# Down's first product evacuated by ScalarE and the residual added later; low parts of weights behind their casts; state sums behind state updates

## The chip, the cores and the metric

The kernel runs on one core of a Trainium2 chip. The metric is the time on the device of one execution of the whole program, in microseconds (us); the median of several runs is taken. A core has five engines, each with its own stream of instructions that it executes in order: TensorE (PE in the profile; its weight loads are PEld), VectorE (DVE), ScalarE (ACT), GpSimd (POOL) and SyncE (SP). Here SP issues nearly all the transfers (DMAs) between the chip's main memory and the on-chip memory SBUF. Matmuls write into PSUM, from where ACT or DVE bring the results back.

## The reference

One layer of a hybrid decoder on 1040 prompt tokens (16 of them learned) and 8 sample tokens, 1048 columns in all, model width 1024, float32:

```
h  = h + 0.5 * swiglu(rmsnorm(h, n1), w1g, w1u, w1d)          # FFN1, hidden width 2816
u  = rmsnorm(h, nm) @ w_in                                    # q, f, i, g (HGRN2); z, x, B, C, dt (Mamba-2)
o  = hgrn2 scan over 4 heads of 128, rms-normed per head, times silu(g)
y  = ssd scan over 8 heads of 64 with state 128, gated by silu(z), rms-normed in two groups
h  = h + concat(o, y) @ w_out
h  = h + 0.5 * swiglu(rmsnorm(h, n2), w2g, w2u, w2d)          # FFN2
y  = rmsnorm(h, norm_final)
swiglu(x, wg, wu, wd) = (silu(x @ wg) * (x @ wu)) @ wd
```

For each of the 8 samples the states of both scans are read, advanced by one token and written out: `h_t = exp(dt A) h + dt x B^T`, `y = h_t C + D x` for the Mamba-2 part, with a state of 512 x 128 per sample.

## The kernel before

**Products.** Every large matmul multiplies float32 numbers as two parts: a high part rounded to fp32r by a cast on ACT, and a low part, the difference, by a subtraction on DVE (`split`, lines 135 to 138). `mm3` (lines 140 to 145) issues three matmuls a product: high by high, high by low, low by high. Columns are handled in quarters of Q = 262.

**The two FFNs** (`ffn`, with `pair` for gate and up, `down` for Down) are written as blocks of 2 x 2 with seven products instead of eight. The seven products are sums and differences of blocks of weights and operands; they are taken in the order 1, 6, 2, 5, 7, 3, 4 in gate and up and 1, 5, 6, 7, 3, 4, 2 in Down. Their order in time is written out by hand: a list of steps (`Steps`), each of which holds some matmuls and perhaps an evacuation after them, and `S.before(i, fn)` puts other work (loads, sums, casts, low parts) ahead of step i in program order. PE, DVE, ACT and SP keep that order here; each engine still runs as far ahead as its waits let it.

*Gate and up.* Each of 22 pairs has 14 steps of 12 matmuls. `Left` prepares its weights: `load` issues four DMAs into tiles of tag "r" (8 buffers), `sum_` makes three sums and differences on DVE, `hi` casts on ACT and `lo` subtracts on DVE into a tile of tag "ws" (6 buffers). `Left.plan` gives the steps, counted from the pair's first: the loads at -10 and -9, the sums at -7 to -5, the split of the i-th product at 2i - 4 (one later for the second pair). `post` evacuates: product 7 makes u1 and multiplies it by the spread factors of the norm (`times_r`, line 445), product 3 does so with g1 and then applies SiLU.

*Hidden.* After every two pairs the hidden blocks and their differences are stored to main memory (`Hidden.jobs`, line 538, tiles of tag "s", 8 buffers).

*Down.* Seven products of 24 steps each: four groups j of 256 output rows, each of three groups g of hidden blocks (4, 4 and 3), each of two halves c. An evacuation follows each j. Operands come back from main memory into tiles of tag "u" (30 buffers; `Hidden.load`: the DMA into the low tile, cast at line 559, low part at line 563), 12 tiles a product, at steps 2, 5, 8, 11, 14 and 17 of the product before. Weights: `pieces` loads 13 steps ahead (line 596), sums 9 ahead (line 606), casts 8 ahead (line 611) and makes the low part 7 ahead (line 616). Six "u" tiles keep sums of weights from product 5 to product 3. The old h of each of the eight row blocks (524 KB) is loaded by `load_h` (line 581) into a tile of tag "s", at steps -4, 2, 8 and 9 for two blocks each, from the copy `xT` in FFN1. `post` adds 0.5 times each finished product to that tile on DVE (line 634). Product 1 goes into all four parts of a j, products 5, 6, 7, 3, 4 and 2 into two, three, two, one, one and one.

Accumulators in the FFNs: two PSUM tiles of two banks each. PE can fill one while the other is evacuated.

**The middle** (input projection, SSM scan, HGRN2 heads, output projection) is not ordered by hand: a scheduler places the instructions by program order and by its own estimate of when they are ready. `ssm_scan` (lines 1075 on) is a chain over nine chunks of 128 tokens; during it PE works at the projections of the first head (`hgrn_project`: q, f, v). Each projected chunk of 350 columns is evacuated by ACT with its function at once: SiLU for q (line 1256), two sigmoids for f (lines 1260 and 1261), a copy for v (line 1266). The scan's own ACT work is Relu and Exp (lines 1111, 1112, 1121). ACT has to load a table of functions when it changes between these sets (ACT_TABLE_LOAD). After each of q, f and v, three jobs are taken from a list: one job per sample (`ssm_samples`), eight of them, and `skip`. A job loads the sample's state, decays it and adds the update on POOL (lines 1191, 1195, 1196), and reduces it against C on DVE (line 1198) right after; then SP stores it (line 1199).

`ssm_norm` squares two tiles on ACT (lines 1231, 1232), adds them on POOL (1233), sums over partitions by matmuls with ones (1237) and scales. For the second group it stands ahead of the output projection's first part (`out_proj`, lines 1459 on), whose operands come back from main memory (line 1718) and are split (lines 137, 138).

Of the kernel before, what the change touches and what calls it, by code (L numbers as in the profile page):

```python
# [17 lines left out]
P = 128  # L18
# [5 lines left out]
NS = 8  # L24
# [318 lines left out]
class Left:  # L343
# [83 lines left out]
def pair(K, S, wg, wu, f, ops, spread, hid, first=None):  # L427
# [20 lines left out]
    def post(p, cs, b):  # L448
        if p == 1:
            nc.scalar.copy(temp("z", cs), b)  # L450
        elif p == 6:
            nc.vector.tensor_add(temp("v", cs), b, temp("z", cs))
        elif p == 2:
            t = times_r("g0", 0, cs, b)
            nc.scalar.activation(t, t, AF.Silu)  # L455
        elif p == 5:
            nc.vector.tensor_add(temp("x", cs), b, temp("v", cs))
        elif p == 7:
            nc.vector.tensor_add(temp("u1", cs), b, temp("x", cs))
            times_r("u1", 1, cs)  # L460
        elif p == 3:
            nc.vector.tensor_add(temp("g1", cs), b, temp("v", cs))
            t = times_r("g1", 1, cs)
            nc.scalar.activation(t, t, AF.Silu)  # L464
        else:
            nc.vector.tensor_add(temp("u0", cs), b, temp("v", cs))
            times_r("u0", 0, cs)
            if "h" not in tm:
                tm["h"] = True
                hid.append(K.slot("s", T))  # L470
            for n in range(2):
                nc.vector.tensor_mul(halves(hid[0][:, n * 2 * Q : n * 2 * Q + 2 * Q])[:, cs], temp(f"g{n}", cs), temp(f"u{n}", cs))
# [8 lines left out]
    def post_first(p, cs, b):  # L481

        if p in (5, 2):
            late[p] = b
        elif p == 7:
            nc.vector.tensor_add(temp("u1", cs), b, temp("x", cs))
        elif p == 3:
            post(2, cs, late[2])
            post(3, cs, b)
            times_r("u1", 1, cs)  # L490
        else:
            post(p, cs, b)
            if p == 6:
                post(5, cs, late[5])
# [77 lines left out]
def down(K, S, wdv, hidden, src, h, after):  # L572
# [576 lines left out]
def ssm_samples(K, a, o):  # L1149
# [34 lines left out]

    def sample(b):
        sb = K.raw().rearrange("p (j n) -> p j n", j=4)
# [5 lines left out]
        for g in range(2):  # L1192
# [3 lines left out]
            nc.gpsimd.tensor_add(sb[:, j2], sb[:, j2], up)  # L1196
            for j in (2 * g, 2 * g + 1):
                nc.vector.tensor_tensor_reduce(up[:, j % 2], sb[:, j], rows[:, 2 + g], 1.0, 0.0, ALU.mult, ALU.add, ys[:, j, b : b + 1])
# [6 lines left out]
    return [lambda b=b: sample(b) for b in range(NS)] + [skip]  # L1205

# [19 lines left out]
def ssm_norm(K, g, tag):  # L1226

    nc = K.nc
    ya, yb = K.y[2 * g], K.y[2 * g + 1]
    v, r = K.slot(tag, w=T), K.slot(tag, w=T)  # L1230
    nc.scalar.activation(v, ya, AF.Square)
    nc.scalar.activation(r, yb, AF.Square)
    nc.gpsimd.tensor_add(v, v, r)
    for c0, w in CHUNKS:
# [13 lines left out]
def hgrn_project(K, a, hd, which, jobs=3):  # L1248
# [9 lines left out]
    def ev_f(c0, w, ps):  # L1258
        f, k = out["f"][:, c0 : c0 + w], out["k"][:, c0 : c0 + w]
        nc.scalar.activation(f, ps, AF.Sigmoid)  # L1260
        nc.scalar.activation(k, ps, AF.Sigmoid, scale=-1.0)
        nc.vector.tensor_scalar(f, f, oml, lb, ALU.mult, ALU.add)
# [302 lines left out]
def body(ctx, tc, a, o):  # L1565
# [130 lines left out]
    for hd in range(NH):  # L1696
        u = hgrn_project(K, a, hd, "qfv")
        pieces = hgrn_scan(K, a, o, hd, u)
        if hd == 0:
            ssm_gate(K, a, 0)  # L1700
            ssm_norm(K, 0, "s")
            for i in range(2):
# [23 lines left out]
    out_proj(K, a, h, 0, opa, 0)  # L1726
    opb = []
# [130 lines left out]
```

## Time and profile before

| | |
|---|---|
| median of 3 runs | 2137.22 us (2134.08 to 2138.86) |
| the profiled execution's own time | 2141.21 us |
| its span, first to last instruction | 2139.4 us |
| mean granted clock of TensorE | 0.975 |
| PE busy | 2021.8 us, 15495 matmuls |
| DVE, ACT, POOL busy | 1491.7, 803.0, 141.3 us |
| HBM read and written | 191.26 and 65.47 MB, 120 GB/s over the span |

Where the stages lie in the span: FFN1's gate and up to 507 us, its Down to about 765, the input projection of the SSM part to about 870, the scan to about 980, the heads to about 1295, the output projection to about 1425, FFN2's gate and up to 1876, its Down to the end.

How to read it. The page gives each engine's busy time and share of the span. A group row (`line engine op out<-in ...`) gives busy time and the mean duration in ns, and behind the second bar the idle time of that engine just ahead of the group with what ended it. A waits row says who waited for whom: us in total, times, the longest. A row by stretches gives from:to, its length, then busy time and number of instructions of PE, PEld, DVE, ACT and POOL, the granted clock, the share of the 16 DMA engines and GB/s. A row of the chain gives start, duration and what ran. Matmuls overlap each other, so the mean duration of one is longer than the distance between two.

### The profile page before, as it was taken

The page shows a single profiled execution, that of the slowest core. Times are in us where ns is not written, and L with a number is a line of the kernel's source. Part 1 is how long each engine was busy: PE and PEld are TensorE (multiplying, and loading weights), DVE is VectorE, ACT ScalarE, POOL GpSimd, SP SyncE. Part 2 cuts the span into 40 slices and gives each one's busy share as a digit, 9 for nine tenths or more (in the row PEclk, how much of TensorE's full clock was granted, in tenths as well). Part 3 has the DMA queues.
Part 4 walks back from the last instruction along what each step waited for, and adds up shares of the span by engine and source line. Part 5 has one row for each costly group of instructions (what it writes and reads, how often), then busy time and mean ns, then how long its engine had stood idle before and what let it go on. Part 6 is the DMA issues. An engine that isn't in the chain of part 4 may idle for free.

```text
span 2139.4 us, 38417 instructions
## 1 busy us (share of the span) xinstructions
PE 2021.8 (95%) x15495; PEld 1965.4 (92%) x15495; DVE 1491.7 (70%) x2489; ACT 803.0 (38%) x1494; POOL 141.3 (7%) x175
## 2 busy tenths in 40 slices
PE   5999999999899899799999998979999999989996
PEld 5999999999899889788989997979999999989996
DVE  6777777777787676596454366677777777778863
ACT  7422222223335443562432335652222222324342
POOL 1000000000002110321111010220000000000000
PEclk8999999999999999999999999999999999999999
DMA  6323333246956511452022053313233242587651
GB/s 189 89 81 100 103 93 105 78 131 228 295 165 194 155 47 31 119 154 75 32 71 79 2 176 107 103 60 106 88 107 105 76 120 81 172 265 230 208 166 59
DMA packets 325033, 259.17 MB, mean 121 GB/s; under 512 B 17712, under 2 KB 301104, under 8 KB 324848
## 3 DMA queue, kind: packets, MB, share of 16 engines
q1 hardware_dynamic: 324616, 256.68, 39.5%
q8 instruction: 122, 2.00, 0.4%
q14 instruction: 55, 0.45, 0.1%
q0 software_dynamic: 224, 0.04, 0.0%
q10 hardware_dynamic: 16, 0.00, 0.0%
HBM read 191.26 MB, written 65.47 MB: 120 GB/s over the span
## 4 chain that ended last, share of the span: by engine, by line
PE 78%; DVE 8%; DMA 6%; ACT 3%; issue 2%; SPq 1%; POOL 1%; DVEq 0%; ACTq 0%; POOLq 0%
PE acc L143 24%; PE acc L144 23%; PE acc L145 23%; DMA r<-in_w_ffn_down_dram 2%; DMA r<-in_w_ffn_up_dram 2%; PE mis L1355 2%; DMA u<-hd 1%; DVE s L634 1%; DVE u L287 1%; DVE r L360 1%; PE mis L1394 0%; PE mis L1450 0%; DVE ws L616 0%; DVE u L298 0%; PE mis L1412 0%
## 5 line engine op out<-in xcount | busy, mean ns | idle before, releaser
L143 PE MATMUL acc<-u,ws 128*128 128x262 f32 (+2 forms) x4504 | 1326.9, 296 | 56.5 <-DVE s L634 20.1
L144 PE MATMUL acc<-u,ws 128*128 128x262 f32 (+2 forms) x4504 | 1315.6, 292 | 0.6 <-DVE u L563 0.3
L145 PE MATMUL acc<-u,ws 128*128 128x262 f32 (+2 forms) x4504 | 1313.9, 292 | 1.0 <-DVE ws L368 0.8
L143 PEld LDWEIGHTS acc<-u,ws 128*128 128x128 f32 x4504 | 858.2, 191 | 75.1 <-issue 21.7
L144 PEld LDWEIGHTS acc<-u,ws 128*128 128x128 f32 x4504 | 862.4, 191 | 2.5 <-DVE u L563 0.7
L145 PEld LDWEIGHTS acc<-u,ws 128*128 128x128 f32 x4504 | 858.3, 191 | 1.9 <-DVE ws L368 1.0
L368 DVE TENSOR_TENSOR ws<-r,ws 128x512 fp32r<-128x512 f32 x308 | 212.0, 688 | 103.7 <-ACT ws L364 103.7
L364 ACT CAST ws<-r 128x512 fp32r<-128x512 f32 x308 | 173.3, 615 | 4.7 <-PE acc L145 3.1
L464 ACT ACTIVATE t<-t 128x524 f32<-128x524 f32 (+1 forms) x46 | 28.6, 622 | 313.1 <-DVE t L445 313.1
L360 DVE TENSOR_TENSOR r<-r,r 128x512 f32<-128x512 f32 x176 | 119.1, 697 | 19.0 <-DMA r<-in_w_ffn_up_dram 17.0
L634 DVE SCALAR_TENSOR_TENSOR s<-acc,s 128x524 f32<-128x524 f32 (+1 forms) x120 | 77.6, 663 | 48.8 <-PE acc L145 47.6
L455 ACT ACTIVATE t<-t 128x524 f32<-128x524 f32 (+1 forms) x46 | 28.7, 623 | 216.7 <-DVE t L445 216.7
L204 POOL TENSOR_TENSOR t<-t,t 128x262 f32<-128x262 f32 x56 | 52.9, 960 | 813.2 <-ACT t L203 813.2
L563 DVE TENSOR_TENSOR u<-u,u 128x1048 fp32r<-128x1048 f32 (+1 forms) x84 | 97.1, 1159 | 8.8 <-ACT u L559 8.8
L445 DVE TENSOR_TENSOR t<-t,u 128x524 f32<-128x524 f32 (+1 forms) x138 | 93.6, 681 | 4.7
L138 DVE TENSOR_TENSOR ws<-r,ws 128x512 fp32r<-128x512 f32 x88 | 60.2, 698 | 39.2 <-ACT ws L137 39.0
L611 ACT CAST ws<-r 128x512 fp32r<-128x512 f32 (+1 forms) x84 | 47.8, 581 | 102.9 <-DVE r L606 39.3
L616 DVE TENSOR_TENSOR ws<-r,ws 128x512 fp32r<-128x512 f32 (+1 forms) x84 | 57.2, 691 | 41.6 <-ACT ws L611 41.5
L611 ACT CAST ws<-u 128x512 fp32r<-128x512 f32 (+1 forms) x72 | 42.1, 585 | 113.2 <-DVE u L606 110.9
L559 ACT CAST u<-u 128x1048 fp32r<-128x1048 f32 (+1 forms) x84 | 83.2, 992 | 2.0 <-DMA u<-hd 2.0
L137 ACT CAST ws<-r 128x512 fp32r<-128x512 f32 x88 | 53.8, 617 | 71.7 <-PE acc L145 51.9
L445 DVE TENSOR_TENSOR t<-acc,u 128x524 f32<-128x524 f32 (+1 forms) x46 | 31.3, 680 | 61.6 <-PE acc L145 61.6
(379 smaller groups left out, 1950.1 us busy)
## 6 DMA issues: line engine op xcount, KB each, us to landing
hd<-s SPq DMA_DIRECT2D x170, 262.0 KB
r<-in_w_ffn_down_dram SPq DMA_DIRECT2D x128, 256.0 KB
u<-hd SPq DMA_DIRECT2D x56, 524.0 KB
r<-in_w_ffn_gate_dram SPq DMA_DIRECT2D x88, 256.0 KB
r<-in_w_ffn_up_dram SPq DMA_DIRECT2D x88, 256.0 KB
r<-in_w_in_dram SPq DMA_DIRECT2D x56, 256.0 KB
r<-in_w_ffn_down_dram SPq DMA_DIRECT2D x64, 192.0 KB
u<-hd SPq DMA_DIRECT2D x28, 393.0 KB
```

The lines of the kernel that those rows point to most:

```text
L138: self.nc.vector.tensor_sub(lo, src, hi.bitcast(F32))
L143: mm(ps, whi, xhi, start=first, stop=False, skip_group_check=more)
L144: mm(ps, whi, xlo, start=False, stop=False, skip_group_check=more)
L145: mm(ps, wlo, xhi, start=False, stop=last, skip_group_check=more)
L360: self.K.nc.vector.tensor_tensor(self.raw[p], self.raw[x], self.raw[y], op)
L364: self.K.nc.scalar.copy(self.w[p][:, : self.n * P], self.raw[p])
L368: self.K.nc.vector.tensor_sub(t[:, 512 : 512 + w], self.raw[p], t[:, :w].bitcast(F32))
L445: nc.vector.tensor_mul(t, t if src is None else src, spread.lanes(i, cs))
L559: K.nc.scalar.copy(hi, lo.bitcast(F32))
L563: K.nc.vector.tensor_sub(lo, lo.bitcast(F32), hi.bitcast(F32))
L611: nc.scalar.copy(w[p, j, g][:, : n * P], src)
L634: nc.vector.scalar_tensor_tensor(t, b, 0.5, t, ALU.mult, ALU.add)
```

## The change

Seven edits.

1. `down`: the eight loads of the old h leave the start. Product 1 writes 0.5 times its result with ACT (`nc.scalar.mul`) into new "s" tiles. The old h of block o is loaded into a "u" tile at Down's step 66 + 5o, and added on DVE at step 74 + 5o, that is 66 to 101 and 74 to 109: product 7 has steps 72 to 95, product 3 steps 96 to 119.
2. `Left.plan`: loads one step earlier; the cast stays where it was, and the low part goes one step later.
3. `pair`: the multiplication of u1 goes from behind product 7 to behind product 3's, also in the first pair.
4. `ssm_samples`: a sample's reductions and store go behind the update of the next sample; nine jobs and `skip`, taken four at a time instead of three for the first head.
5. `hgrn_project`, first head: q and f are copied raw out of PSUM chunk by chunk, and the functions run once over all 1048 columns after the third chunk. In `ev_f` the two sigmoids change places.
6. `ssm_norm` ends in a function of its own (`ssm_norm_end`).
7. `out_proj` can call a function after its first quarter (`mid`); the second group's norm is ended there. The first group's is ended at once, as before.

```diff
     def plan(self, S, s0, late):
         for ps, ds, fn in (
-            ((1, 7, 4, 2), (-10, -10, -9, -9), self.load),
+            ((1, 7, 4, 2), (-11, -11, -10, -10), self.load),
             ((5, 6, 7, 3), (-7, -7, -6, -5), self.sum_),
-            (ORDER, [2 * i - 4 + late for i in range(7)], self.split),
+            (ORDER, [2 * i - 4 + late for i in range(7)], self.hi),
+            (ORDER, [2 * i - 3 + late for i in range(7)], self.lo),
         ):
...
         elif p == 7:
             nc.vector.tensor_add(temp("u1", cs), b, temp("x", cs))
-            times_r("u1", 1, cs)
         elif p == 3:
             nc.vector.tensor_add(temp("g1", cs), b, temp("v", cs))
             t = times_r("g1", 1, cs)
             nc.scalar.activation(t, t, AF.Silu)
+            times_r("u1", 1, cs)
...
-    def load_h(o):
-        t = K.slot("s", T)
-        nc.sync.dma_start(t, src(o))
-        h.append(t)
-        hs.append(t.rearrange("p (c n t) -> p c n t", c=2, n=2))
+    def tiles(j):
+        for _ in range(2):
+            h.append(K.slot("s", T))
+            hs.append(h[-1].rearrange("p (c n t) -> p c n t", c=2, n=2))
+
+    def residual(o, at):
+        box = []
+
+        def load():
+            box.append(K.slot("u", T))
+            nc.sync.dma_start(box[0], src(o))
+
+        S.before(at - 8, load)
+        S.before(at, lambda: nc.vector.tensor_add(h[o], h[o], box[0]))
 
     for o in range(KT):
-        S.before(s0 + (-4, 2, 8, 9)[o // 2], lambda o=o: load_h(o))
+        residual(o, s0 + 74 + 5 * o)
...
     def post(p, j, cs, b):
-        for i, n in {1: ((0, 0), (0, 1), (1, 0), (1, 1)), 5: ((0, 1), (1, 1)), 6: ((0, 1), (1, 0), (1, 1)), 7: ((1, 0), (1, 1)), 3: ((0, 1),), 4: ((1, 0),), 2: ((0, 0),)}[p]:
+        if p == 1:
+            tiles(j)
+            for i in range(2):
+                for n in range(2):
+                    nc.scalar.mul(hs[2 * j + i][:, cs, n], b, 0.5)
+            return
+        for i, n in {5: ((0, 1), (1, 1)), 6: ((0, 1), (1, 0), (1, 1)), 7: ((1, 0), (1, 1)), 3: ((0, 1),), 4: ((1, 0),), 2: ((0, 0),)}[p]:
...
-    def sample(b):
+    state = {}
+
+    def update(b):
...
-            for j in (2 * g, 2 * g + 1):
-                nc.vector.tensor_tensor_reduce(up[:, j % 2], sb[:, j], rows[:, 2 + g], 1.0, 0.0, ALU.mult, ALU.add, ys[:, j, b : b + 1])
+        state[b] = sb, rows
+
+    def output(b):
+        sb, rows = state.pop(b)
+        junk = K.t(4 * P).rearrange("p (j n) -> p j n", j=4)
+        for j in range(4):
+            nc.vector.tensor_tensor_reduce(junk[:, j], sb[:, j], rows[:, 2 + j // 2], 1.0, 0.0, ALU.mult, ALU.add, ys[:, j, b : b + 1])
         nc.sync.dma_start(ov[0, b], sb)
+
+    def sample(b):
+        if b < NS:
+            update(b)
+        if b > 0:
+            output(b - 1)
...
+    def ev_raw(x):
+        left = [3]
+
+        def ev(c0, w, ps):
+            nc.scalar.copy(out[x][:, c0 : c0 + w], ps)
+            left[0] -= 1
+            if left[0] == 0:
+                (ev_q if x == "q" else ev_f)(0, T, out[x])
+
+        return ev
...
+    if hd == 0:
+        evs.update(q=ev_raw("q"), f=ev_raw("f"))
...
-def out_proj(K, a, h, part, ops, half, after=None):
+def out_proj(K, a, h, part, ops, half, after=None, mid=None):
...
+        if u == 1 and mid:
+            mid()
...
-        u = hgrn_project(K, a, hd, "qfv")
+        u = hgrn_project(K, a, hd, "qfv", 4 if hd == 0 else 3)
...
-    ssm_norm(K, 1, "u")
+    norm1 = ssm_norm(K, 1, "u")
...
-    out_proj(K, a, h, 0, opa, 0)
+    out_proj(K, a, h, 0, opa, 0, mid=norm1)
```

More of the change, by code (lines that the diff above doesn't have):

```diff
@@ L484, in post_first @@
             late[p] = b
-        elif p == 7:
-            nc.vector.tensor_add(temp("u1", cs), b, temp("x", cs))
         elif p == 3:
@@ L489, in post_first @@
             post(3, cs, b)
-            times_r("u1", 1, cs)
         else:
@@ L1203, in skip @@
             nc.vector.scalar_tensor_tensor(xs[j][:, TP:T], xs[j][:, TP:T], K.dcol[:, j : j + 1], ys[:, j], ALU.mult, ALU.add)
-    return [lambda b=b: sample(b) for b in range(NS)] + [skip]
+    return [lambda b=b: sample(b) for b in range(NS + 1)] + [skip]
 def ssm_gate(K, a, g):
@@ L1226, in ssm_norm, with ssm_norm_end @@
 def ssm_norm(K, g, tag):
-    nc = K.nc
     ya, yb = K.y[2 * g], K.y[2 * g + 1]
     v, r = K.slot(tag, w=T), K.slot(tag, w=T)
-    nc.scalar.activation(v, ya, AF.Square)
-    nc.scalar.activation(r, yb, AF.Square)
-    nc.gpsimd.tensor_add(v, v, r)
+    K.nc.scalar.activation(v, ya, AF.Square)
+    K.nc.scalar.activation(r, yb, AF.Square)
+    K.nc.gpsimd.tensor_add(v, v, r)
+    return lambda: ssm_norm_end(K, g, v, r)
+def ssm_norm_end(K, g, v, r):
+    nc = K.nc
     for c0, w in CHUNKS:
@@ L1259, in ev_f @@
         f, k = out["f"][:, c0 : c0 + w], out["k"][:, c0 : c0 + w]
+        nc.scalar.activation(k, ps, AF.Sigmoid, scale=-1.0)
         nc.scalar.activation(f, ps, AF.Sigmoid)
-        nc.scalar.activation(k, ps, AF.Sigmoid, scale=-1.0)
         nc.vector.tensor_scalar(f, f, oml, lb, ALU.mult, ALU.add)
@@ L1700, in body @@
             ssm_gate(K, a, 0)
-            ssm_norm(K, 0, "s")
+            ssm_norm(K, 0, "s")()
             for i in range(2):
```

## The prediction

> **What bounds the kernel now.** I read the page's busy line, its slices and its chain first, then the waits of PE, then PE's busy time by stage.
>
> ```profile
> span 2139.4 us, 38417 instructions
> PE 2021.8 (95%) x15495; PEld 1965.4 (92%) x15495; DVE 1491.7 (70%) x2489; ACT 803.0 (38%) x1494; POOL 141.3 (7%) x175
> ...
> PE   5999999999899899799999998979999999989996
> ...
> DMA  6323333246956511452022053313233242587651
> ...
> PE 78%; DVE 8%; DMA 6%; ACT 3%; issue 2%; SPq 1%; POOL 1%; DVEq 0%; ACTq 0%; POOLq 0%
> ```
>
> PE is the bound, and all that can be won without taking matmuls away is where it waits. The DMA slices have their high digits at 9 to 11 and 35 to 36: the start of Down in each FFN. Who makes PE wait, in total us, times, longest:
>
> ```profile
> PE acc L143 <- DVE s L634: 21.9, 10, 5.4
> ...
> PE acc L143 <- DVE t L457: 8.2, 7, 6.3
> PE mis L1118 <- DVE s L1114: 7.6, 2, 6.2
> ...
> PE mis L1104 <- DVE s L1125: 5.6, 2, 5.2
> ...
> PE mis L1237 <- POOL u L1233: 4.7, 1, 4.7
> ...
> PE acc L143 <- ACT u L1256: 2.0, 1, 2.0
> ...
> PE acc L143 <- ACT u L1266: 1.7, 1, 1.7
> ...
> PE acc L143 <- DVE t L462: 1.2, 2, 0.6
> ```
>
> L634 is Down's evacuation; L1104 to L1125 are the SSM scan, L1256 and L1266 the first head's projection, L1237 the second SSM norm. Now the busy time by stage. The first row is products 1 and 5 of FFN1's Down, the next three its products 6, 7 and 3; then products 1 and 5 of FFN2, its product 3, and the scan:
>
> ```profile
> 507.50:583.50 76.00, 68.11 (x531) 67.11 (x532) 55.74 (x82) 25.03 (x37) 0.00 (x0) 0.96 0.89 276
> 583.50:615.50 32.00, 32.00 (x265) 32.00 (x264) 27.17 (x42) 12.41 (x18) 0.00 (x0) 1.00 0.54 164
> 615.50:647.50 32.00, 32.00 (x264) 32.00 (x263) 26.81 (x40) 12.42 (x18) 0.00 (x0) 1.00 0.67 207
> 647.50:679.50 32.00, 32.00 (x265) 32.00 (x264) 24.67 (x32) 17.24 (x32) 10.02 (x10) 1.00 0.55 167
> 1875.80:1951.50 75.70, 68.75 (x533) 67.81 (x534) 55.90 (x82) 25.04 (x37) 0.00 (x0) 0.95 0.91 278
> ...
> 2015.50:2047.50 32.00, 32.00 (x265) 32.00 (x264) 22.08 (x32) 14.02 (x21) 0.00 (x0) 1.00 0.67 208
> 880.00:950.00 70.00, 53.67 (x361) 48.06 (x362) 52.74 (x142) 46.09 (x97) 30.57 (x39) 0.90 0.64 185
> ```
>
> A product is 24 steps of 11 matmuls on the average, 264, and takes 32.0 us where nothing is late: 0.121 us a matmul, 1.33 us a step. Products 1 and 5 should take 64.0 us. They take 76.0 and 75.7, of which 3 and 5 matmuls (1.0 us) belong to the neighbours: 22.7 us are lost in the two Downs. PE's idle time is less than that; the granted clock (0.96 and 0.95, against 1.00) is the rest.
>
> Why they are lost, in the stretch 507.5 to 560, by groups, by SP's waits and by the chain:
>
> ```profile
> L143 PE MATMUL acc<-u,ws 128*128 128x262 f32 x113 | 33.5, 297 | 8.1 <-DVE s L634 7.1 <-DVE t L462 0.6 <-ACT ws L611 0.4
> L634 DVE SCALAR_TENSOR_TENSOR s<-acc,s 128x524 f32<-128x524 f32 x16 | 10.9, 700 | 0.3
> L616 DVE TENSOR_TENSOR ws<-r,ws 128x512 fp32r<-128x512 f32 (+1 forms) x9 | 5.7, 643 | 12.1 <-ACT ws L611 12.1
> L611 ACT CAST ws<-r 128x512 fp32r<-128x512 f32 (+1 forms) x9 | 4.9, 582 | 23.3 <-DMA r<-in_w_ffn_down_dram 15.4 <-PE acc L145 7.9
> ...
> SPq L538 <- DVE s L472: 12.1, 1, 12.1
> ...
> 529.70 10.03 DMA r<-in_w_ffn_down_dram
> ...
> s<-xT SPq DMA_DIRECT2D x8, 524.0 KB
> ```
>
> PE waits for L634 (7.1 of 8.1), L634 stands on DVE behind a low part L616, L616 waits for its cast L611, and L611 for a weight's DMA, one of which took 10.03 us for 192 or 256 KB. It stands in line behind the eight residual loads of 524 KB, six of which leave after SP has been held for 12.1 us by the last pair's store.
>
> **The change, part by part.**
>
> *Down's first product.* Out of the start go 8 x 524 KB = 4.2 MB, at 276 GB/s 15 us of transfers, six eighths of it just ahead of the late weights. DVE loses 16 evacuations of 700 ns (10.9 us). ACT gets them; the nearest row, a copy of the same 128x524 from PSUM, is
>
> ```profile
> L450 ACT COPY t<-acc 128x524 f32<-128x524 f32 x17 | 10.2, 597 | 43.6 <-PE acc L145 43.6
> ```
>
> 16 x 0.6 = 9.6 us over product 1, where ACT's own work is about the 12.4 us of the rows of products 6 and 7: it hides. The new waits: evacuations queue on ACT behind casts that wait for weights. A weight of a step s is cast 8 steps (10.7 us) ahead, and PE has two accumulators, so an evacuation may be 8 us late. With 3.1 MB fewer ahead of them (11 us at 276 GB/s) the weights that landed 10 us after issue land in 2 to 5. SP's wait of 12.1 us stays. Of the 22.7 us I leave 1.1 in each Down, for product 5, whose weights come two at a time: -20.5. Ends: 0 and -22.7.
>
> The Trainium skill speaks against this move: "ScalarE: Activation LUTs", Rules for kernel authors, puts mul and add on VectorE. The row disagrees for this shape: ACT 597 ns, DVE 700 ns. At three times DVE's 700 ns, the page's largest ratio, the 16 would be an estimated 34 us, more than product 1 lasts, and the gain would be gone; I go by the row.
>
> *Residual in products 7 and 3.* The eight loads now leave at steps 66 to 101 of Down, eight steps ahead of eight adds at 74 to 109. The add's nearest row is two SBUF operands of 128x1048:
>
> ```profile
> L287 DVE TENSOR_TENSOR u<-u,u 128x1048 f32<-128x1048 f32 x8 | 10.0, 1244 | 0.0
> ```
>
> 9.9 us, 6.2 of it in product 7. DVE has 26.81 of 32 us there: 33.0, over full. But it now idles 0.8 us between a weight's sum and its low part, for ACT's cast, and each add falls between these two; so it falls some 2 us behind, and PE bears up to 8 less the 1 to 2 us that the evacuations trail now. Product 3 has 24.67 + 3.7. Transfers: 207 and 167 GB/s plus 4.2 MB in 47 us (90 GB/s) is below the 276 at which product 5 runs. Buffers: tag "u" has 30 slots. Two products' operands (24) and the kept sums (6) fill them by step 65, so the load at 66 holds SP until PE has done step 66, and with it the weights behind; the operand loads at 86 and 89 are held likewise. SP's lead is set by freed slots already. A weight is loaded 13 steps ahead of PE; held for two, it is still on time. I take +0.5 in each Down, +1.0; ends 0 and the second rival.
>
> *FFN pairs.* Loads go one step (1.33 us) earlier, low parts one step later, still three steps ahead of PE; eight "r" slots hold the seven or eight live ones. DVE's sums wait for a load in 21 pairs:
>
> ```profile
> DVE r L360 <- DMA r<-in_w_ffn_up_dram: 17.0, 21, 1.6
> ```
>
> at most 1.6, so nearly all goes, but PE feels only 8.2 - 6.3 = 1.9 us of it (the 6.3 is FFN2's first pair): -1.5, ends -1.9 and +1. times_r of u1 now follows product 3's g1, so the accumulator that PE wanted at Down's first step is read 0.7 us sooner: L462's 1.2 us go, -1.2. DVE's saved waits for casts lie beside PE: nothing.
>
> *SSM.* Head 0's q and f leave PSUM by copies, with one SiLU and two sigmoids afterwards. Rows of 880 to 950:
>
> ```profile
> L1112 ACT ACT_TABLE_LOAD x4 | 5.1, 1283 | 0.1
> ...
> L1256 ACT ACT_TABLE_LOAD x2 | 2.6, 1283 | 0.0
> L1260 ACT ACT_TABLE_LOAD x2 | 2.6, 1283 | 0.0
> ...
> L1266 ACT COPY u<-acc 128x350 f32<-128x350 f32 x2 | 0.9, 438 | 0.0
> ...
> DVE t L1198 <- POOL r L1196: 9.1, 2, 7.3
> ```
>
> Nine loads (with L1121's) fall to about four: five x 1.283 = 6.4 us off ACT; against it six copies (2.6) and three long calls (3.2) for nine short ones (4.1): 4.7 us net. The Trainium skill ("ScalarE: Activation LUTs", Rules for kernel authors) budgets 2.7 us a switch; by that it would be 11.8 and the whole sum 7 us better; here the row decides. The state sums L1198 move behind the next state's update, so DVE should not stand 7.3 us for POOL. SP's store of each state moves with them. PE's waits here are 7.6 + 5.6 + 2.0 + 1.7 = 16.9. This part isn't ordered by hand, so I take half of the two longest (6.2 and 5.2): -6, ends -16.9 and +6.2 (one more such wait).
>
> *Second norm.* The ones-matmuls go behind the first quarter of the output projection. PE's wait, the norm's six matmuls and the low parts that the quarter needs:
>
> ```profile
> 1297.24 3.59 PE L1237 MATMUL mis<-u,ones 128*128 128x350 f32 x6 [4.70 <-POOL u L1233]
> 1298.21 1.43 DVE u L138 x4
> ```
>
> PE waits from 1292.5 to 1297.2. The first low part is there near 1298.7, so without the norm in front PE would wait about 6 us instead of 4.7, less what ACT and DVE gain by the norm's absence: 0, ends -4.7 and +2.
>
> **Sum.** -20.5 + 1.0 - 1.5 - 1.2 - 6 + 0 = -28.2. The profiled execution took 2141.2: 2113. The median of the three runs is 4.0 lower, so 2109.
>
> **Rivals.** *The first product keeps its waits* (0.10): SP's 12.1 us hold is the cause, and ACT now waits for the weights in DVE's place. For it: the hold stays. Against: DMA runs full after the hold, and most of that is residual. 2109 + 20.5 = 2130, or 2134 if products 7 and 3 pay 2 each.
>
> *Products 7 and 3 pay* (0.17, slower). SP is held for "u" slots at steps 66, 86 and 89, and the weights behind it come late while DVE is full. Price: three waits as long as L634's longest, 5.4; in products 1 and 5 8.1 us of idle time cost 12, so 24 us a Down, 48 - 29 = +19: 2156. It decides from 16.8 us a Down (gains 29.2 and 0.2%, 4.3, halved). Against: product 5 ran with 0.89 DMA share and little loss.
>
> *The scan is ordered worse* (0.09): +6.2 and +2 for -6 and 0: 2123.
>
> **Chances.** The forecast has 0.64. A change of 0.2% (4 us) is about what a measurement can tell. Faster: 0.64 + 0.09 + 0.04 of the first rival = 0.77; same 0.06; slower 0.17. Range: 2094 (the middle at its better ends) to 2138 (both lesser rivals in, the slower one out); the likeliest case alone is 2098 to 2122.
>
> **What would show it.** Right: in Down's products 1 and 5 PE takes about 65 us with granted clock near 1.00, and no weight load takes 10 us; products 7 and 3 stay at 32 each though DVE shows 33 busy; ACT has about four table loads in the scan; PE waits less for L1114 and L1125. Wrong: PE waiting in products 7 or 3 for L634, or SP's longest waits being the residual's; PE waiting for ACT's new evacuation; new scan waits of 5 us.

## The result, and the profile after

The changed kernel takes 2105.28 us (median of four runs, 2096.91 to 2113.13) against 2138.04 for the kernel before on the same chip: a ratio of 0.9843, 95% interval 0.9818 to 0.9868, a gain of 28 to 39 us. Its profiled execution took 2105.23 us, 36.0 less than the one before.

Lines have moved: Down's evacuation L634 is now L647 (product 1's on ACT is L643), the weights' load, sum, cast and low part are L603, L613, L618 and L623, the operand's load, cast and low part L553, L557 and L561, the residual's load and addition L587 and L590. In the scan L1114 and L1125 are L1127 and L1138; the norm's sum and matmul L1258 and L1267.

The page of the changed kernel:

```profile
span 2103.5 us, 38460 instructions
...
PE 2004.5 (95%) x15495; PEld 1951.0 (93%) x15495; DVE 1492.9 (71%) x2469; ACT 819.4 (39%) x1524; POOL 144.7 (7%) x175
...
DMA  6223233336967511452022053313242333487851
```

PE runs the same 15495 matmuls. Its busy time fell by 17.3 us, its idle time by 18.6 (117.6 to 99.0 as span less busy time). A matmul takes less time when the granted clock is higher, and part of the busy time that was won goes with the waits: in Down's products 1 and 5, over both Downs, PE's idle time fell by 14.8 us and its busy time by 7.0, at a granted clock of 0.96 and 0.95 before and 1.00 after. The other 10 us of busy time were won in other stages, most of which the change does not touch; there the clock differs from run to run (see the last paragraph on the prediction). The DMA slices at Down's start (9 to 11, and 35 to 36) are still the fullest.

Who makes PE wait, in total us, times, longest:

```profile
PE acc L143 <- DVE s L647: 9.1, 6, 2.5
...
PE mis L1131 <- DVE s L1127: 7.3, 3, 5.2
...
PE acc L143 <- DVE t L458: 6.6, 2, 6.4
PE mis L1267 <- POOL u L1258: 4.7, 1, 4.7
...
PE acc L143 <- ACT u L1296: 2.6, 1, 2.6
PE acc L143 <- ACT u L1305: 2.0, 1, 2.0
...
PE acc L144 <- DVE u L561: 1.7, 2, 1.2
PE mis L1117 <- DVE s L1138: 1.2, 1, 1.2
```

Down's evacuation went from 21.9 to 9.1 us; the six waits left lie in its last product, which the change did not touch. The 6.4-us wait of FFN2's first pair and the norm's 4.7 us stand as they were, and L462's 1.2 us are gone. In the scan PE waits 8.5 us for the two lines that cost 13.2; nearly all of the fall is L1138's (5.6 to 1.2), while L1127's 7.3 us are close to the 7.6 of before, and the waits for the first head's copies rose from 3.7 to 4.6.

By stretches (length, busy time and count of PE, PEld, DVE, ACT, POOL, clock, DMA share, GB/s): products 1 and 5 of FFN1's Down; its products 7 and 3; products 1 and 5 of FFN2; its product 3:

```profile
504.16:568.50 64.34, 64.34 (x531) 64.34 (x529) 45.31 (x66) 33.68 (x53) 0.00 (x0) 1.00 0.94 271
600.70:632.85 32.15, 32.15 (x266) 32.15 (x265) 28.22 (x41) 11.90 (x17) 0.00 (x0) 1.00 0.73 236
632.85:666.46 33.61, 32.37 (x266) 32.16 (x265) 29.64 (x38) 15.15 (x29) 9.48 (x8) 1.00 0.70 225
1850.20:1914.80 64.60, 64.60 (x530) 64.57 (x529) 45.95 (x67) 33.82 (x53) 0.00 (x0) 1.00 0.92 274
1979.20:2012.00 32.80, 32.38 (x266) 32.17 (x265) 29.25 (x41) 14.52 (x22) 0.00 (x0) 1.00 0.81 260
```

Products 1 and 5 now hold no idle time and run at full clock. Product 3 has 1.24 us of idle time in FFN1 and 0.42 in FFN2.

Where the time went in this and the following kernels. A stage is measured from its first matmul to the next stage's first, so that all kernels are cut at the same matmul; the scan alone is measured from its first transposition to the first of its last group. Each column is one profiled execution; times in us.

| stage | before | after | Down alone | pairs alone | middle alone | loads back | DVE evacuates |
|---|---|---|---|---|---|---|---|
| FFN1 gate and up, without first pair | 434.8 | 431.8 | 435.0 | 432.2 | 435.5 | 433.1 | 433.0 |
| FFN1 Down, product 1 | 40.7 | 32.3 | 32.3 | 40.8 | 41.3 | 40.9 | 33.1 |
| product 5 | 34.9 | 32.1 | 32.1 | 34.9 | 34.9 | 32.2 | 36.4 |
| products 7 and 3 | 64.4 | 65.7 | 65.6 | 64.4 | 64.4 | 65.9 | 64.4 |
| scan | 105.3 | 102.2 | 104.7 | 104.0 | 99.2 | 101.1 | 98.3 |
| FFN2 gate and up, without first pair | 433.9 | 432.2 | 434.5 | 434.3 | 435.7 | 432.1 | 432.8 |
| FFN2 Down, product 1 | 40.3 | 32.2 | 32.4 | 40.5 | 40.5 | 39.6 | 32.4 |
| product 5 | 34.9 | 32.4 | 32.4 | 34.9 | 34.9 | 32.5 | 35.1 |
| products 7 and 3 | 64.4 | 65.0 | 65.3 | 64.4 | 64.4 | 65.6 | 64.8 |

### The profile page after: what moved, and what is told of

Its sections match the earlier page's. It is cut to its first block, busy times and chain, and to the rows that moved or that the text cites. A ratio compares the mean times of both kernels' runs of the same rounds, so it can differ in the third digit from the quotient of the medians.

```text
span 2103.5 us, 38460 instructions
## 1 busy us (share of the span) xinstructions
PE 2004.5 (95%) x15495; PEld 1951.0 (93%) x15495; DVE 1492.9 (71%) x2469; ACT 819.4 (39%) x1524; POOL 144.7 (7%) x175
## 4 chain that ended last, share of the span: by engine, by line
PE 79%; DVE 11%; ACT 4%; DMA 3%; issue 2%; SPq 1%; POOL 1%; DVEq 0%; ACTq 0%; POOLq 0%
PE acc L143 24%; PE acc L145 23%; PE acc L144 23%; PE mis L1398 1%; DVE u L561 1%; DVE ws L623 1%; DVE s L647 1%; DVE s L590 1%; DVE r L613 1%; DVE u L287 1%; PE mis L1437 0%; DVE s L1400 0%; DVE u L298 0%; DVE s L1412 0%; DVE u L613 0%
## 5 line engine op out<-in xcount | busy, mean ns | idle before, releaser
L143 PE MATMUL acc<-u,ws 128*128 128x262 f32 (+2 forms) x4504 | 1322.8, 295 | 39.7 <-ACT t L451 9.8
L145 PE MATMUL acc<-u,ws 128*128 128x262 f32 (+2 forms) x4504 | 1311.2, 291 | 0.9 <-DVE ws L368 0.8
L143 PEld LDWEIGHTS acc<-u,ws 128*128 128x128 f32 x4504 | 854.7, 190 | 55.8 <-ACT t L451 10.5
L145 PEld LDWEIGHTS acc<-u,ws 128*128 128x128 f32 x4504 | 854.3, 190 | 2.1 <-DVE ws L368 1.3
L561 DVE TENSOR_TENSOR u<-u,u 128x1048 fp32r<-128x1048 f32 (+1 forms) x84 | 97.8, 1167 | 9.1 <-ACT u L557 9.1
L647 DVE SCALAR_TENSOR_TENSOR s<-acc,s 128x524 f32<-128x524 f32 (+1 forms) x88 | 55.8, 649 | 39.7 <-PE acc L145 39.0
L557 ACT CAST u<-u 128x1048 fp32r<-128x1048 f32 (+1 forms) x84 | 83.3, 993 | 1.4 <-DMA u<-hd 1.4
L618 ACT CAST ws<-u 128x512 fp32r<-128x512 f32 (+1 forms) x72 | 42.1, 585 | 101.0 <-DVE u L613 98.2
L623 DVE TENSOR_TENSOR ws<-r,ws 128x512 fp32r<-128x512 f32 (+1 forms) x84 | 57.7, 698 | 32.2 <-ACT ws L618 32.1
L618 ACT CAST ws<-r 128x512 fp32r<-128x512 f32 (+1 forms) x84 | 47.5, 581 | 71.5 <-DVE r L613 30.6
```

The source lines that it names most:

```text
L143: mm(ps, whi, xhi, start=first, stop=False, skip_group_check=more)
L145: mm(ps, wlo, xhi, start=False, stop=last, skip_group_check=more)
L557: K.nc.scalar.copy(hi, lo.bitcast(F32))
L561: K.nc.vector.tensor_sub(lo, lo.bitcast(F32), hi.bitcast(F32))
L618: nc.scalar.copy(w[p, j, g][:, : n * P], src)
L623: nc.vector.tensor_sub(t[:, 512 : 512 + n * P], box[0], t[:, : n * P].bitcast(F32))
```

## The experiments

**The three parts, each alone.** Down's edit alone, in the kernel before:

```diff
-        S.before(s0 + (-4, 2, 8, 9)[o // 2], lambda o=o: load_h(o))
+        residual(o, s0 + 74 + 5 * o)
...
+                    nc.scalar.mul(hs[2 * j + i][:, cs, n], b, 0.5)
```

> Only Down's edit (product 1 out by ACT, residual loaded and added amid products 7 and 3). Theory (the residual's transfers made the weights late): products 1 and 5 take about 64 to 65 us in both Downs instead of 75 to 76, products 7 and 3 together at most 2 us more a Down: 20 us faster than the kernel before, ratio near 0.991. Rival (the gain needs the other edits too, or comes from the granted clock): products 1 and 5 stay above 70 us, ratio 0.996 or more.

Measured: 2114.63 us, ratio 0.9884 (0.9865 to 0.9903), 21 to 29 us faster. Products 1 and 5 lose 21.6 us over both Downs, products 7 and 3 gain 2.0.

The pairs' edits alone:

```diff
-            ((1, 7, 4, 2), (-10, -10, -9, -9), self.load),
+            ((1, 7, 4, 2), (-11, -11, -10, -10), self.load),
...
-            (ORDER, [2 * i - 4 + late for i in range(7)], self.split),
+            (ORDER, [2 * i - 4 + late for i in range(7)], self.hi),
+            (ORDER, [2 * i - 3 + late for i in range(7)], self.lo),
...
-            times_r("u1", 1, cs)
...
+            times_r("u1", 1, cs)
```

> Only the pairs' edits (loads a step earlier, low parts a step later, u1's multiplication behind product 3). Theory: gate and up of FFN1 and of FFN2 get 3 and 1.6 us shorter, the two Downs keep 75 to 76 us in products 1 and 5: 3 to 5 us faster, ratio 0.998. Rival (the low parts come late for PE): gate and up the same or longer, ratio 1.000 or more.

Measured: 2134.84 us, ratio 0.9964 (0.9952 to 0.9977), 5 to 10 us faster. In the trace the pairs of FFN1 are 2.6 us shorter, those of FFN2 0.4 longer. One trace can't place the gain: over the kernels with these edits FFN1's pairs took 431.6 to 434.1 us, without them 434.8 to 436.6.

The middle's edits alone (state sums, raw copies, second norm):

```diff
+    def sample(b):
+        if b < NS:
+            update(b)
+        if b > 0:
+            output(b - 1)
...
+    if hd == 0:
+        evs.update(q=ev_raw("q"), f=ev_raw("f"))
...
+    out_proj(K, a, h, 0, opa, 0, mid=norm1)
```

> Only the middle's edits (state sums behind updates, raw copies of q and f, the second norm ended behind a quarter of the output projection). Theory: the scan from its first to its last transposition gets 3 us shorter, the norm's place the same; the rest of the 8 us that the middle lost between the two profiles is the granted clock: 2 to 4 us faster, ratio 0.998 to 0.999. Rival (all 8 us come from these edits): ratio 0.996.

Measured: 2135.40 us, ratio 0.9977 (0.9963 to 0.9991), 2 to 8 us faster. The norm's wait is still 4.7 us. The three gains, 24.8, 7.7 and 4.9 us, make 37.4; the whole change gave 33.6, with some 5 us of uncertainty. Within that the parts add up.

**Are the early loads the cause in Down?** The changed kernel, with eight residual loads issued again at their old steps into the same "s" tiles; product 1 then overwrites them:

```diff
+    def early(o):
+        h.append(K.slot("s", T))
+        hs.append(h[-1].rearrange("p (c n t) -> p c n t", c=2, n=2))
+        nc.sync.dma_start(h[-1], src(o))
...
+    for o in range(KT):
+        S.before(s0 + (-4, 2, 8, 9)[o // 2], lambda o=o: early(o))
```

> The changed kernel with the eight residual loads issued a second time, at the old steps and into the same tiles, ahead of ACT's evacuation, which overwrites them; everything else stays. Theory (transfers): products 1 and 5 of each Down go back to 72 to 76 us, the kernel to about 2123 to 2127, ratio 0.994. Rival (the gain came from taking the evacuation off DVE): products 1 and 5 stay at 64 to 66 us, ratio 0.985.

Measured: 2122.50 us, ratio 0.9920 (0.9902 to 0.9938). By stretches, products 1 and 5 of FFN1 and of FFN2; then a wait; then the chain of the stretch 503 to 548, by line, and one of its pieces:

```profile
503.45:544.36 40.91, 35.21 (x266) 34.79 (x265) 19.21 (x26) 17.55 (x29) 0.00 (x0) 0.92 0.85 261
544.36:576.55 32.19, 32.19 (x264) 32.19 (x265) 25.81 (x39) 16.08 (x25) 0.00 (x0) 1.00 1.05 309
1857.10:1896.72 39.62, 34.22 (x267) 33.79 (x265) 19.21 (x26) 17.55 (x29) 0.00 (x0) 0.96 0.85 269
1896.72:1929.18 32.46, 32.46 (x264) 32.46 (x265) 26.07 (x39) 16.25 (x25) 0.00 (x0) 1.00 1.05 309
```

```profile
PE acc L143 <- ACT s L644: 5.7, 2, 3.1
```

```profile
by line: DMA r<-in_w_ffn_down_dram 22.1%; DMA u<-hd 20.0%; DMA s<-xT 12.9%; ACT u L557 6.6%; issue 6.3%; ACT s L644 6.3%; SPq L536 4.2%; PE acc L143 3.3%; DVE t L446 3.2%; DVE s L473 3.0%; PE acc L144 2.4%; PE acc L145 2.4%; DVE u L615 1.6%
...
529.61 9.95 DMA r<-in_w_ffn_down_dram
```

In the changed kernel the chain of 500 to 560 holds no transfer at all:

```profile
by line: PE acc L143 33.5%; PE acc L144 32.4%; PE acc L145 32.3%; DVE ws L623 1.1%; DVE t L460 1.0%; issue 0.2%
```

With the loads back, a weight takes 10 us again, product 1 takes 40 us again, and PE waits for ACT's evacuation (L644 here) in DVE's place, since it stands on ACT behind casts of operands and weights that landed late (an operand's load took 9.02 us). ACT's evacuation itself did not wait for the load into its tile; what it waited for was PE (4.2 us). Product 1's 16.0 of the 21.8 us have come back. Product 5 stays at 32 us although the transfers run at 309 GB/s beside it: its 5.3 us have another cause. One is seen in the chain of the kernel before, at the last place in FFN1's product 5 where PE waits. Three evacuations L634 stand on DVE ahead of an operand's low part L563, and PE goes on when that is done:

```profile
554.99 1.33 DVE s L634 x2
...
556.96 0.98 DVE u L563
...
557.99 0.40 PE acc L144
```

PE's idle time in that product is only 0.33 us, at a granted clock of 0.93. But the clock does not seem to set its time: in the five kernels here that keep the old Down it lasts 34.9 us in both FFNs, whether PE idles 0.0 or 1.1 us of it.

**Is it the engine that evacuates?** The changed kernel with product 1 evacuated by DVE:

```diff
-                    nc.scalar.mul(hs[2 * j + i][:, cs, n], b, 0.5)
+                    nc.vector.tensor_scalar(hs[2 * j + i][:, cs, n], b, 0.5, None, ALU.mult)
```

> The changed kernel, with Down's first product evacuated by VectorE (a multiplication by 0.5, no residual) where ScalarE did it. Theory (the eight residual loads were what held Down's first and fifth products; which engine evacuates does not matter): product 1 and product 5 of both Downs stay at 32 to 33 us each, and the ratio to the kernel before is that of the changed kernel, 0.984 to 0.987. Rival (ScalarE's share of the evacuation is what freed product 5, whose 2.7 us per Down did not come back when the loads were put back): product 5 returns to about 35 us in each Down, or product 1 stays over 33, some 5 us in all, and the ratio is about 0.987 to 0.989.

Measured: 2109.47 us, ratio 0.9856 (0.9838 to 0.9874). Product 5 by stretch, PE's wait in it, and DVE's work around it:

```profile
536.98:573.38 36.40, 33.94 (x265) 33.73 (x266) 30.89 (x47) 13.72 (x21) 0.00 (x0) 0.95 0.95 285
```

```profile
PE acc L144 <- DVE u L561: 2.5, 1, 2.5
```

```profile
542.99 2.79 DVE L643 TENSOR_SCALAR s<-acc 128x524 f32<-128x524 f32 x4
545.70 0.97 DVE L561 TENSOR_TENSOR u<-u,u 128x786 fp32r<-128x786 f32 x1
```

The rival holds for product 5: four evacuations of 0.7 us stand on DVE ahead of an operand's low part that PE is waiting for. Product 5 costs 7.0 us more over both Downs, product 1 1.0 more, product 3 1.6 less, for a reason that is not shown. The net is some 6 us in the stages, 3 a Down; the ratios, with intervals that overlap, neither show nor deny it. So by the stages of these traces moving product 1 to ACT and moving the loads are two gains: 16 us by the transfers, about 5 by DVE's relief.

**What do products 7 and 3 pay for?** The changed kernel without the late loads and additions, so that the old h is missing from both Downs' results:

```diff
-    for o in range(KT):
-        residual(o, s0 + 74 + 5 * o)
```

> The changed kernel without the sixteen late residual loads and additions of the two Downs: the old h is then missing from the output of both feed-forward layers. Theory (products 7 and 3 pay for these loads and additions, and for nothing else): the gaps of TensorE in FFN1's product 3 (1.24 us) and in FFN2's (0.42 us) go, products 3 come back from 33.6 and 32.8 to 32.1 to 32.3 us, and 1.5 to 2.5 us are gained against the changed kernel: a ratio of about 0.983 to the kernel before. Rival (product 3 is longer for another reason, its low-part splits and evacuations on VectorE): the two gaps stay and so does the time. Second rival (the additions also hold other work that the gaps don't show): more than 4 us are gained.

Measured: 2106.57 us, ratio 0.9839 (0.9816 to 0.9862). Products 3 by stretch go back to 32.15 us, without idle time:

```profile
633.61:665.76 32.15, 32.15 (x266) 32.15 (x265) 24.72 (x34) 17.23 (x32) 9.38 (x10) 1.00 0.52 159
```

So by the traces the late residual costs PE 1.9 us in all and no more, which is too little for the two ratios to show. Is it the slots or DVE? SP's waits in the changed kernel, 585 to 665, show the slot holds that the prediction's slower rival spoke of:

```profile
SPq L553 <- DVE s L590: 11.2, 2, 10.6
SPq L587 <- PE acc L144: 10.6, 2, 10.1
```

A later kernel (the better version below, with each residual tile loaded four steps ahead of its addition where it stood eight ahead) takes most of them away:

```diff
-        S.before(at - 8, load)
+        S.before(at - 4, load)
```

> The kernel with the output projection's operands split between the chunks of the gate, and Down's eight late residual loads issued four steps ahead of their additions where they stood eight ahead, so that each tile is held for about 5 us less. Theory (slots held by the residual tiles are what delays product 3's operand and makes TensorE wait 1.26 and 0.16 us for L561): both gaps fall below 0.3 us, SyncE's longest waits for L587 and L553 fall by some 5 us, products 3 take 32.2 to 32.6 us, 1 us is gained at most, ratio 0.981. Rival (VectorE is full in product 7 and that delays the low part, whatever the slots do): the gap in FFN1's product 3 stays at 1.0 us or more. Against both: a residual load that lands late makes VectorE wait for a transfer, and products 7 and 3 grow by 2 us or more.

Measured: 2101.67 us, ratio 0.9826 (0.9804 to 0.9848). SP's waits in 560 to 670, and PE's in 600 to 667:

```profile
SPq L587 <- DVE s L590: 7.5, 2, 6.8
...
SPq L553 <- DVE s L590: 2.8, 1, 2.8
```

```profile
PE acc L144 <- DVE u L561: 1.3, 1, 1.3
```

The hold of the operand's load L553 fell from 10.6 to 2.8 us, and PE's wait stayed. The theory of the slots fell; the full DVE delays the low part. The changed kernel's trace agrees: DVE works without a pause from 626.90 to 641.26, two of the additions among its work, the low part L561 comes last, at 640.29, and PE's wait for it ends at 641.31.

**The additions on GpSimd**, to empty DVE:

```diff
-        S.before(at, lambda: nc.vector.tensor_add(h[o], h[o], box[0]))
+        S.before(at, lambda: nc.gpsimd.tensor_add(h[o], h[o], box[0]))
```

> The changed kernel with the sixteen residual additions of the two Downs on GpSimd, where VectorE did them. Nearest row: GpSimd adds 128x1048 in 2.4 us, VectorE in 1.24. Theory (TensorE's gaps in products 3, 1.24 and 0.42 us, came from VectorE being full, not from the slots that hold the loads): the gaps go or fall below 0.3 us, products 3 take 32.2 to 32.6 us, SyncE's waits for slots stay at about 10 us, and 1 to 2 us are gained, which is less than the comparison of the times can show. Rival (the held loads are the cause): GpSimd holds the slots longer, the gaps stay or grow, and evacuations on VectorE wait for GpSimd.

Measured: 2136.94 us, ratio 0.9999 (0.9983 to 1.0015): all of the gain is lost. The theory missed; the rival had the gaps grow, for the held slots, but what the rows show first is DVE stopped by GpSimd. Products 7 and 3 of FFN1 by stretch, then GpSimd's and DVE's instructions in order of time, then DVE's weight sum of 128x384 by group in the changed kernel, 600 to 666:

```profile
599.52:638.41 38.89, 32.95 (x266) 32.30 (x265) 33.53 (x40) 12.38 (x18) 11.87 (x5) 1.00 0.70 230
638.41:678.01 39.60, 36.12 (x264) 35.44 (x265) 32.16 (x35) 15.81 (x30) 16.59 (x11) 0.92 0.49 155
```

```profile
615.83 2.78 POOL L590 TENSOR_TENSOR s<-s,u 128x1048 f32<-128x1048 f32 x1 [10.82 <-DVE s L647]
624.74 3.33 POOL L590 TENSOR_TENSOR s<-s,u 128x1048 f32<-128x1048 f32 x1 [6.13 <-DVE s L647]
```

```profile
616.21 2.81 DVE L613 TENSOR_TENSOR r<-r,u 128x384 f32<-128x384 f32 x1
...
624.52 1.24 DVE L561 TENSOR_TENSOR u<-u,u 128x1048 fp32r<-128x1048 f32 x1
625.68 2.94 DVE L623 TENSOR_TENSOR ws<-r,ws 128x512 fp32r<-128x512 f32 x1
```

```profile
L613 DVE TENSOR_TENSOR r<-r,u 128x384 f32<-128x384 f32 x3 | 1.7, 551 | 0.0
```

GpSimd runs from 615.83 to 618.61; the DVE sum that starts at 616.21 and should take 0.55 us ends at 619.02. The second addition starts while DVE is at L561, until 625.76, and lasts 3.33 us, 0.55 longer than the first (L1258, an addition of that shape in the norm of the changed kernel, takes 2.41); the low part that follows on DVE, of 0.69 us, ends only 0.55 us after GpSimd. Whoever comes second waits. An addition cost DVE 1.24 us, and on GpSimd it blocks DVE for over 2. The Trainium skill ("SBUF — State Buffer", SBUF: two separate sides) says that the two engines share a pair of ports as an exclusive lock, which a DVE operation with two SBUF inputs also takes against a GpSimd operation that reads SBUF, and that the loser fully blocks; these rows agree. The lock is not shown to be all of the loss: the gaps hold 4.5 us of waits for ACT's operand casts (L557) too, and SP was held for GpSimd's slots (8.6 us for L587, 4.4 for L553); how much each cost is open.

**Which of the scan's edits counts?** In the kernel before, the state sums alone, then the raw copies alone:

```diff
-    return [lambda b=b: sample(b) for b in range(NS)] + [skip]
+    return [lambda b=b: sample(b) for b in range(NS + 1)] + [skip]
```

> The kernel before with one of the scan's edits alone: the sample's output sums on VectorE stand one sample behind its updates. Theory (VectorE's wait of 7.3 us for GpSimd is what cost the scan): that wait is gone, the activation table loads in the scan stay at 13, the scan is 2 to 5 us shorter than the 105.3 of the kernel before, and the ratio is 0.998 to 0.999. Rival (the raw copies with their fewer table loads carry the gain): the scan stays at 104 to 106 us and the ratio is 1.000.

```diff
+    if hd == 0:
+        evs.update(q=ev_raw("q"), f=ev_raw("f"))
```

> The kernel before with another of the scan's edits alone: head 0's q and f leave PSUM by plain copies, with SiLU and the sigmoids called once afterwards. Theory (the sample sums carried the scan's gain; the copies take two table loads off ScalarE, which was not what the scan waited for): 11 table loads in the scan, VectorE's wait of 7.3 us for GpSimd still there, the scan at 103 to 106 us, ratio 0.999 to 1.001. Rival (the table loads do count): the scan is 2 to 4 us shorter and the ratio 0.998.

Measured: the sums 2135.77 us, ratio 0.9983 (0.9966 to 1.0000); the copies 2134.82 us, ratio 0.9987 (0.9973 to 1.0001). The scan by stretch in the kernel before, after, with the sums alone and with the copies alone:

```profile
872.98:978.32 105.34, 88.28 (x615) 79.31 (x614) 79.64 (x202) 66.74 (x140) 33.61 (x42) 0.94 0.47 135
```

```profile
856.61:958.76 102.15, 88.80 (x615) 79.08 (x614) 82.96 (x200) 65.35 (x138) 35.81 (x42) 0.93 0.48 139
```

```profile
874.11:973.00 98.89, 85.26 (x606) 75.61 (x604) 84.30 (x203) 65.86 (x139) 37.22 (x42) 0.95 0.48 143
```

```profile
868.03:969.50 101.47, 88.73 (x614) 79.71 (x613) 81.32 (x200) 65.01 (x138) 35.27 (x42) 0.93 0.48 140
```

The sums alone do what was expected of DVE's wait and of the 13 table loads, and shorten the scan by 6.4 us, more than the 2 to 5 expected. The copies alone shorten it by 3.9 us with 11 loads, as the rival had it (2 to 4). But that doesn't show that the loads count: DVE's wait for POOL fell to 1.8 us as well, without the sums' edit,

```profile
DVE t L1198 <- POOL r L1196: 1.8, 1, 1.8
```

so that wait is a matter of when the jobs fall, and either edit moves it. Over nine profiles with all middle edits the scan took 97.7 to 102.4 us, mean 99.8; over three without, 104.0 to 105.3: about 5 us are won. How they divide between the two edits stays open: by its ratio each alone is worth between nothing and some 6 or 7 us.

**The second norm, and a better version.** The changed kernel's wait of 4.7 us stayed because the products that were to fill it had no operands: their tiles still held the input of the second gate. With eight tiles of their own, loaded and split ahead of that gate:

```diff
+    opa = [(K.slot("u", T, F32R), K.slot("u", T, F32R)) for i in range(4)]
...
+            K.split(t, hi[:, cs], lo[:, cs])
     ssm_gate(K, a, 1)
...
-    opa = [(K.xhi[i], K.xlo[i]) for i in range(4)]
```

> The changed kernel, with the first operands of the output projection in eight tiles of their own, loaded and split ahead of the second gate, where they were put into the tiles of the normalized input that the second gate's projection still read. Theory (the second norm's edit gave nothing since the 32 instructions that it put later had no operands that were ready to go ahead): TensorE's wait of 4.7 us for GpSimd's sum ahead of the second norm is filled by the first products of the output projection, and the time falls by 4 to 6 us, ratio about 0.982. Rival (the order on TensorE is set by something else, so the wait stays): 4.7 us are still spent there, and the time is the changed kernel's.

Measured: 2108.14 us, ratio 0.9835 (0.9812 to 0.9857), no better than the change. The norm's wait is gone, and a longer one has come in the gate. PE's wait, and ACT's work ahead of it:

```profile
PE acc L143 <- ACT t L1243: 10.2, 1, 10.2
```

```profile
1263.57 0.48 ACT L137 CAST u<-t 128x348 fp32r<-128x348 f32 x1 [2.11 <-DMA t<-mspill]
1264.07 1.28 ACT L1243 ACT_TABLE_LOAD   x1
1265.36 0.46 ACT L1243 ACTIVATE t<-acc 128x350 f32<-128x350 f32 x1
```

The gate's SiLU, which frees PE's accumulator, stands on ACT behind casts that wait for loads. So the loads and splits of each chunk go behind that chunk's two SiLU calls:

```diff
-def ssm_gate(K, a, g):
+def ssm_gate(K, a, g, after=None):
...
+        if after:
+            after(c)
...
-    ssm_gate(K, a, 1)
+    ssm_gate(K, a, 1, operands)
```

> As the kernel with the output projection's first operands in eight tiles of their own, but with the loads and splits of each chunk between the chunks of the second gate, behind that chunk's two SiLU calls on ScalarE, where the other kernel put all of them ahead of the gate. Theory (the 10.2 us that TensorE waited there for L1243 were the SiLU calls standing on ScalarE behind casts of loaded operands; it is the place of the casts, not the tiles, that cost): the 10.2-us wait goes, the 4.7-us wait for GpSimd's sum stays away, and the time is 4 to 8 us below the changed kernel's: ratio 0.980 to 0.983. Rival (the loads come too late for any place before the gate's end, behind tiles that VectorE frees late): a wait of 4 us or more comes back in the gate or ahead of the norm, and the time is the changed kernel's, 0.984.

Measured: 2099.39 us, ratio 0.9813 (0.9791 to 0.9835). The stretch that holds both waits:

```profile
1240.00:1286.00 46.00, 44.60 (x302) 41.60 (x302) 34.50 (x54) 30.66 (x51) 2.45 (x1) 1.00 0.44 150
```

PE idles 1.4 us in these 46: the 4.7-us and the 10.2-us wait are both gone. The last 1296 matmuls of the large products (L143 to L145) ahead of FFN2 take 256.1 us from the first on, for 264.6 in the changed kernel, 10.1 of them idle for 16.0. The version is faster than the kernel before. By the medians it is about 6 us faster than the change too, but these intervals overlap a little, so that this rests on the trace, where both waits are gone.

## Why the prediction came out right, step by step

*Down's first product*, -20.5: the stages measured -21.8 (-11.3 and -10.6). The mechanism was as told: the chain holds no transfer, ACT's longest wait for a weight there is 4.7 us, and SP's hold at Down's start (its waits in 485 to 560) is still there and costs PE nothing:

```profile
SPq L536 <- DVE s L473: 21.5, 2, 13.5
```

Two corrections. The prediction's fear that ACT's evacuation queues behind casts came true only with the loads put back (5.7 us of PE's waits). And it gave the loss to the loads as a whole and kept back 1.1 us a Down for product 5; the runs point to DVE for product 5's 5.3 us, which went with the 16 evacuations: they stayed away with the loads put back, and came back, with PE waiting for DVE, when DVE evacuated product 1. ACT's evacuation was costed at 597 ns by the nearest row; in the stretch 500 to 552 of the changed kernel it is

```profile
L643 ACT ACTIVATE s<-acc 128x524 f32<-128x524 f32 x16 | 9.3, 606 | 4.5 <-PE acc L145 4.3
```

and DVE took 700 ns when it did them, so the row decided rightly against the rule of the Trainium skill ("ScalarE: Activation LUTs", Rules for kernel authors) that puts a multiplication on VectorE. That page gives its ratio of up to about 3 for bf16; these tiles are float32.

*Products 7 and 3*, +1.0: +1.9. The holds of SP came as the slower rival had them, 10.1 and 10.6 us, and cost PE nothing that shows, although the prediction had put them among the signs of being wrong; what PE does pay for is the step's own other half, DVE being full. The rival failed at its price: it let three holds of SP cost three waits of PE, and the weights stayed far enough ahead.

*Pairs*, -1.5 and -1.2: L462's 1.2 us went. The rest was sized too small: the edits alone gave 5 to 10 us, for 2.7. Where the surplus lies is open, since in their one trace only FFN1's pairs are shorter.

*Scan*, -6: about -5, by a different route. The step that failed is the count of table loads, nine to about four. In the stretch that answers to the prediction's there are seven, since the scheduler puts the scan's Exp between the two sigmoids and each call loads its own table:

```profile
910.35 1.28 ACT L1134 ACT_TABLE_LOAD   x1 [0.24 <-DMA s<-cumd]
...
913.25 1.28 ACT L1291 ACT_TABLE_LOAD   x1
```

Of the 6.4 us off ACT two loads, 2.6 us, are real, and ACT's busy time in the scan fell by 1.4 only. DVE's 7.3-us wait for POOL went, as told. PE does wait less for L1138, but not for L1127, which the prediction had named as well.

*Second norm*, 0: 0, for the reason given, and the experiments show it: with operands that are ready the wait goes.

*Sum*: -28.2 forecast, 33.6 measured by the ratio. The stages' terms that the edits touched come to -21.8 + 1.9 - 4.9 (pairs, with the first ones of both FFNs) - 3.2 = -28.0, just the forecast. That it fits so closely is in part luck: the pairs and Down's first product gave more than forecast, the scan in this profile and products 7 and 3 less. The other 8 us between the two profiles lie for the most part in stages that the change doesn't touch and that differ from run to run with the granted clock: the heads took 312.9 us before at 0.973, 308.2 after at 0.988, and 305.8 at 0.994 with Down's edit alone.

## What to carry to other kernels

A late weight at the start of a stage is first a question of what was put into the same transfer queue ahead of it: moving 4.2 MB a Down that nobody needed yet to a later stage won more here than any work on the engines. When a helper instruction is moved to another engine, look at what then stands behind it in that engine's order: the sixteen evacuations of product 1 cost nothing that shows on ACT and some 3 us a Down on DVE, by the stages of one trace each, and casts that wait for loads must not stand ahead of the instruction that frees an accumulator. Waits of the issuing queue of 10 us and more were no cost here; follow such a wait to PE before pricing it.

## What was not expected of the hardware

GpSimd is no free helper for DVE: an addition of 128x1048 on GpSimd (2.8 and 3.3 us in the rows above) stopped a DVE operation with two SBUF operands until GpSimd was done (551 ns became 2.8 us), and with sixteen such additions products 7 and 3 of the two Downs took 27 us more (78.5 and 79.3 us for 65.7 and 65.0). The kernel before had shown it already: beside GpSimd's 10.02 us of other work in FFN1's product 3, DVE's 32 instructions took 24.67 us, and the same number in FFN2's, where GpSimd rests, 22.08; the low part L616 of 128x512 took 848 ns in the first and 689 in the second.

A wait can cost more than its length: in Down's products 1 and 5 PE's idle time fell by 14.8 us and its busy time, for the same matmuls, by 7.0 besides. With the loads put back and 5.7 and 5.4 us of idle time in product 1, it ran at a granted clock of 0.92 and 0.96, against 1.00 without. That the waits lower the clock is argued from these pairs of numbers; no experiment changed the one without the other.
